# A recurrence whose first step loads into memory of its own, with late loads moved to another queue

## The chip, the core and the metric

The kernel runs on one core of one Trainium2 chip. The metric is the device time of one execution in microseconds (us); less is better. Before the change the median of 3 runs is 937.24 us (936.47 to 937.66).

Engines are named as in the profile: PE (TensorE), PEld (its weight load), DVE (VectorE), ACT (ScalarE), POOL (GpSimd), SP (SyncE). SP and POOL each issue transfers in the order in which their own instructions stand; an instruction that waits holds up all that stand behind it on its engine.

## What is computed

One layer of an encoder trunk over 512 tokens of width 1024, in float32. The pieces that matter here are the two branches and how they merge:

```python
h = rmsnorm(x); u = h @ w_in          # columns: RWKV-7 | differential attention | two gates
# branch A: one delta-rule scan per direction, 8 heads of 64
def step(state, inp):
    r_t, w_t, k_t, v_t, kk_t, a_t = inp
    sa = einsum('bhij,bhj->bhi', state, -kk_t)
    state = state * w_t + sa[..., None] * (kk_t * a_t) + v_t[..., None] * k_t
    return state, einsum('bhij,bhj->bhi', state, r_t)
y = scan(forward) + scan(reverse)     # then group norm, bonus, gate, projection -> A
# branch B: (softmax(Q1 K1) - lam * softmax(Q2 K2)) V, per-head norm, projection -> B
x = x + (sigmoid(gate_a) * A + sigmoid(gate_b) * B) @ w_out
x = x + relu(rmsnorm(x) @ w_ff1)**2 @ w_ff2
x = x + sigmoid(rmsnorm(x) @ w_pg) * (p @ w_pp)
out = rmsnorm(x)
```

## The kernel before

Every dense product is made in three passes of split operands (high times high, low times high, high times low), so a weight block of 512 KB is loaded (`raw`, line 127), split by ACT into `whi` (L131) and by DVE into `wlo` (L135), and used by 24 matmuls of 128x512 (L245 to L247, or L655 where PE's order is chained by hand). The blocks stream through three `raw` buffers on SP's queue in the order of a list.

The stages follow each other: projections and the preparation of the scans; differential attention; the scans, which the code calls the sequence; the merge (`ya`, then `wout`); the two feed-forward products; the last gate and norm. Stages that leave PE waiting are filled with dense matmuls of gates: `gA` in the attention, `gB` in the sequence.

The scan is done in chunks of 64 tokens, 8 per direction, so the sequence has 8 steps `i`, each with the two directions `d` side by side; direction 1 walks the chunks backwards. A step needs three loads from DRAM, all on POOL's queue: `sga` (1 MB, made by `chunk`, L916 to L921), `stt` (the 64x64 inverses of 8 heads, 128 KB, L1032) and `srv` (the values, in partitions 64 to 127 of a tile whose lower half the step fills in later, L1034). The inverses are completed late: `corner_blocks` (L872 to L912) makes their corner blocks on PE in the last part of the attention and writes them to DRAM (`td<-z`, L912), four small writes for each direction.

Within a step (`step`, L1045 to L1098) PE forms `al` from `sga` and the values (and, from the second step on, the state `S`); ACT and DVE copy it to `B` (L1059, L1060); PE multiplies by the inverses into `ss` (L1066); ACT and DVE copy that into the lower half of `srv` (L1067, L1068); PE makes the update of the state (`ss<-srv,sga`) and the output (`yy`), which DVE and ACT carry into `S` and `ya`. After the first stage of each step one half of a `gB` block (12 matmuls) is put in between, and in the first step one half more behind `B`.

Memory decides when a load may start. Pools are stacked on two sides. The tiles of the attention lie in the pool `at`, which is given up when the attention's last product, the projection `yb` of its output (high part `oTh`, low part `oTl`), has read them; `yp` and `seq` (`sq_` in the code) are opened after `at` is closed, on the same side and so in its memory. Each direction has a `tt` and an `rv` tile of its own in `sq_`, two deep, allocated by `slot` (L1025). `kq` and `kq2` lie on the other side: `kq` holds `kT` and later the `k` tile of the chunks, `kq2` (opened at tile `t == 10` of the attention's loop) one chunk buffer.

Loads of three other things wait for their turn on SP's queue between the weight blocks: `bvt` (1 MB, L1138), `g2` (256 KB, L1159) and eight `gA` gates (256 KB each, L1203), which the merge needs; the `gA` tile has three buffers, so the fourth load waits for the first tile's last reader.

Of the kernel before, what the change touches and what calls it, by code (L numbers as in the profile page):

```python
# [10 lines left out]
F32 = mybir.dt.float32  # L11
F32R = mybir.dt.float32r
# [4 lines left out]
P = 128  # L17
# [61 lines left out]
def moved(a):  # L79

    return a.rearrange("p (h t) -> p t h", h=2)
# [28 lines left out]
class Weights:  # L110
# [34 lines left out]
    def next(self, *key):  # L145
        assert UNITS[self.cur] == key, (UNITS[self.cur], key)
        self.prefetch(1 + self.AHEAD)
        w = self.ready[self.cur]
        self.ready[self.cur] = None
        self.cur += 1  # L150
        return w
# [3 lines left out]
def tile_hybrid_encoder(ctx, tc, xT, wts, par, cst_a, cst_p, lor, lqk, nfin, out, dbg=None):  # L155
# [492 lines left out]
    def chained(f, *args, **kw):  # L648

        nonlocal last_pe  # L650
        if last_pe is None:
            last_pe = f(*args, **kw)
        else:
            with tc.issue_after(last_pe.ins):
                last_pe = f(*args, **kw)  # L655
# [81 lines left out]
    def gates():  # L737
        for f in range(GE, GA0):
            yield from gate(f, at, range(8))

        for f2 in range(4):
            wh, wl = W.next("dao", f2)
            for i in range(2):
                ps = psd.tile([P, T], F32, tag="d", name=f"yb{f2}{i}")
                for k in range(4):
                    wk = slice(k * 256 + i * P, k * 256 + i * P + P)
                    for j, (a, b) in enumerate(((wh, oTh), (wh, oTl), (wl, oTh))):
                        chained(nc.tensor.matmul, ps, a[:, wk], moved(b[:, k, :]), start=(k == 0 and j == 0), stop=(k == 3 and j == 2))
                    if k == 3:
                        if not mB:  # L750
                            mB.extend(gp.tile([P, 4, T], F32, tag=f"m{j}", name=f"mB{j}", bufs=1) for j in range(2))
                        nc.scalar.activation(mB[f2 // 2][:, 2 * (f2 % 2) + i, :], ps, AF.Copy)
                    yield
# [3 lines left out]
    def fillk(n, wait=False):  # L757
        nonlocal done
        for _ in range(n):
            if done >= 8 * (GA0 - GE) + 32:  # L760
                return
            next(early_gates)
            done += 1
            if not wait:
                gated()
# [146 lines left out]
                nc.gpsimd.dma_start(tdb[g, 0:H, vs, H:C], x_[rows[g]])  # L912

    early = {}

    def chunk(i, d):  # L916

        own, tag = (kq, "hl"[d] + str(i % 3)) if i % 3 < 2 else ((kq2, "h2"), (kq, "k"))[d]
        ga = own.tile([P, 4, 512], F32, tag=tag, name=f"sga{i}{d}", bufs=1)
        nc.gpsimd.dma_start(ga, gad[d * NCH + (i if d == 0 else NCH - 1 - i)])  # L920
        return ga  # L921

    corners = corner_blocks()
    o_ = at.tile([P, 4, T], F32, tag="qk", name="o_", bufs=1)
# [4 lines left out]
    for t in range(NT + 1):  # L929
        if t > 2:  # L930
            values((t - 3) // 2, (0, 1) if t % 2 == 1 else (2, 3))
        if t + 3 < NT:
            scores(t + 3)
        fillk(AFS[t] if done < AFT else 0, True)
        if t > 0:
            turned(t - 1)
        if t + 2 < NT:
            exps(t + 2)
        if t + 1 < NT:
            weigh(t + 1)  # L940
        if t < NT:
            turn(t)
        gated()
        if t in EC:
            if t == EC[-1]:
                kq2 = pool("kq2")
            for d in range(1 if t == EC[-1] else 2):
                early[EC.index(t), d] = chunk(EC.index(t), d)
        next(diag, None)
        if t == CT:  # L950
            next(corners)
    W.AHEAD = AH2
    fillk(AF2)
    values(NT // 2 - 1, range(4))
    fillk(AF3)
# [23 lines left out]
    selb = at.tile([4, 4, P], F32R, tag="e1", name="selb", bufs=3)  # L979
    nc.scalar.activation(selb, ident[0:4, 0:4, None].broadcast_to([4, 4, P]), AF.Copy)  # L980
    oTh = at.tile([P, 4, T], F32R, tag="q", name="oTh", bufs=1)
    oTl = kq.tile([P, 4, T], F32R, tag="k", name="oTl", bufs=1)
    for hd in range(4):
        ps = psm.tile([P, T], F32, tag="sc", name=f"rb{hd}", bufs=4)
        for i, t_ in enumerate((roh, rol)):
            chained(nc.tensor.matmul, ps, selb[:, hd, :], t_, start=(i == 0), stop=(i == 1))
        on = at.tile([P, T], F32, tag="e0", name=f"on{hd}", bufs=3)
        nc.vector.scalar_tensor_tensor(on, o_[:, hd, :], sub8, ps, ALU.mult, ALU.mult)
        nc.scalar.activation(oTh[:, hd, :], on, AF.Copy)
        nc.vector.tensor_tensor(oTl[:, hd, :], on, oTh[:, hd, :].bitcast(F32), ALU.subtract)  # L990

# [28 lines left out]
            with tc.issue_after(seq_last.ins):  # L1022
                seq_last = nc.tensor.matmul(*args, **kw)  # L1023

    def slot(kind, shape, i, d, n):  # L1025
        return sq_.tile(shape, F32, tag=f"{kind}{d}{i % n}", name=f"s{kind}{i}{d}", bufs=1)

    def load(i, d):
        c = i if d == 0 else NCH - 1 - i
        ga = early.pop((i, d), None) or chunk(i, d)  # L1030
        tt_ = slot("tt", [C, 8, C], i, d, 2)
        nc.gpsimd.dma_start(tt_, tdv[d * NCH + c])  # L1032
        rv = slot("rv", [P, 8, C], i, d, 2)
        nc.gpsimd.dma_start(rv[C:P].rearrange("p u e -> p (u e)"), vd[c * C:(c + 1) * C])  # L1034
        return ga, tt_, rv


# [2 lines left out]
    S = [sq_.tile([P, 4, 2, C], F32, name=f"S{d}") for d in range(2)]  # L1040
    for d in range(2):
        nc.gpsimd.memset(S[d], 0.0)
    early[2, 1] = chunk(2, 1)

    def step(i, d):  # L1045

# [8 lines left out]
            for p, hh in units:  # L1055
                seq_mm(al[half(hh), p, :], ga[:, p, 384:448], S[d][:, p, hh, :], start=False, stop=(p == 3))
        yield
        B = sq_.tile([C, 4, 2, C], F32, tag=f"B{d}", name=f"B{i}{d}", bufs=1)
        nc.scalar.activation(B[:, :, 0, :], al[half(0)], AF.Copy)  # L1059
        nc.vector.tensor_copy(B[:, :, 1, :], al[half(1)])  # L1060
        yield
# [71 lines left out]
    dense = dense_work()  # L1133
    for i in range(NCH):
        steps = [step(i, d) for d in range(2)]
        if i == NCH // 2:
            with tc.issue_after(W.sent.ins):
                nc.sync.dma_start(bvt, bvd.rearrange("a q t -> q a t"))  # L1138
        for st_ in range(6):
            for g in steps:  # L1140
                next(g)
            if st_ == 0 or (i, st_) == (0, 2):
                fill(1)
    pss.close_()
    sq_.close_()
    kq2.close_()
# [7 lines left out]
    mean = sq_.tile([P, 4, 8], F32, name="mean")  # L1154
    var = sq_.tile([P, 4, 8], F32, name="var")
    g2 = sq_.tile([P, 512], F32, name="g2")
    sent = W.sent.ins
    with tc.issue_after(sent):
        nc.sync.dma_start(g2, lor[:, 2, :])  # L1159
    gps = []  # L1160
    yps = [psm.tile([P, T], F32, tag="m", name=f"yps{p}") for p in range(4)]
    for tt in range(4):
# [32 lines left out]
    for f2 in range(4):  # L1195
        w = W.next("wo", f2)
        for i in range(2):
            f = 2 * f2 + i
            ps = psd.tile([P, T], F32, tag="d", name=f"ya{f}")
            dense_fm(w, ps, 4, ygh, ygl, f0=i * P, fw=256)  # L1200
            gA = yp.tile([P, T], F32, tag="gA", name=f"gAt{f}", bufs=3)
            with tc.issue_after(sent):
                nc.sync.dma_start(gA, gad_[f])  # L1203
            nc.vector.scalar_tensor_tensor(gA, gA, 1.0, ps, ALU.add, ALU.mult)
            nc.vector.tensor_tensor(gA, gA, mB[f // 4][:, f % 4, :], ALU.add)
            dump("mg", gA, f)
            nc.scalar.activation(halves(mh[:, f, :]), turns(gA), AF.Copy)
            nc.vector.tensor_tensor(halves(ml[:, f, :]), turns(gA), halves(mh[:, f, :].bitcast(F32)), ALU.subtract)
# [276 lines left out]
```

## Time and profile before

| | before |
|---|---|
| median of 3 runs | 937.24 us (936.47 to 937.66) |
| the profiled execution: its own time / its span | 939.69 us / 937.9 us |
| PE busy, PEld busy | 884.5 us (94%), 741.7 us (79%) |
| DVE, ACT, POOL busy | 570.4 us (61%), 431.0 us (46%), 51.7 us (6%) |
| mean granted clock of PE | 0.976 of full speed |
| chain that ended last: PE, DVE, ACT, issue, DMA | 65%, 15%, 8%, 5%, 5% |
| moved by SP's queue, by POOL's queue | 114.09 MB, 23.60 MB |

The span is what the profiler saw between the first and the last instruction. An execution's own time is 1.8 us longer here, and the profiled execution is 2.45 us above the median of the runs. Busy time says which engine has work; the chain that ended last says what the end waited for, step by step.

### The profile page before, as it was taken

The page shows a single profiled execution, that of the slowest core. Times are in us where ns is not written, and L with a number is a line of the kernel's source. Part 1 is how long each engine was busy: PE and PEld are TensorE (multiplying, and loading weights), DVE is VectorE, ACT ScalarE, POOL GpSimd, SP SyncE. Part 2 cuts the span into 40 slices and gives each one's busy share as a digit, 9 for nine tenths or more (in the row PEclk, how much of TensorE's full clock was granted, in tenths as well). Part 3 has the DMA queues.
Part 4 walks back from the last instruction along what each step waited for, and adds up shares of the span by engine and source line. Part 5 has one row for each costly group of instructions (what it writes and reads, how often), then busy time and mean ns, then how long its engine had stood idle before and what let it go on. Part 6 is the DMA issues. An engine that isn't in the chain of part 4 may idle for free.

```text
span 937.9 us, 14083 instructions
## 1 busy us (share of the span) xinstructions
PE 884.5 (94%) x5640; PEld 741.7 (79%) x5640; DVE 570.4 (61%) x873; ACT 431.0 (46%) x677; POOL 51.7 (6%) x74
## 2 busy tenths in 40 slices
PE   5899898999999996899999999999999999999995
PEld 3788777788567785788877888888888888888884
DVE  7756999769985521467897665554354445334453
ACT  6665555453577531332464544542153235213555
POOL 5000000010000012322000000000000000000000
PEclk9989999999899997899999999999999999999998
DMA  5534788795245258586125423232323232323502
GB/s 214 186 113 146 255 262 265 246 372 164 90 151 123 81 145 244 169 292 209 33 80 192 143 90 104 99 109 94 110 93 113 90 113 90 113 91 111 201 25 90
DMA packets 65553, 138.58 MB, mean 148 GB/s; under 512 B 25808, under 2 KB 28112, under 8 KB 63184
## 3 DMA queue, kind: packets, MB, share of 16 engines
q1 hardware_dynamic: 61248, 114.09, 37.3%
q0 software_dynamic: 4240, 23.60, 7.5%
q8 instruction: 44, 0.72, 0.3%
q14 instruction: 21, 0.17, 0.1%
HBM read 106.73 MB, written 30.93 MB: 147 GB/s over the span
## 4 chain that ended last, share of the span: by engine, by line
PE 65%; DVE 15%; ACT 8%; issue 5%; DMA 5%; SPq 1%; POOL 0%; POOLq 0%; DVEq 0%; ACTq 0%
PE f L246 12%; PE f L247 12%; PE f L245 12%; PE gA L655 4%; DVE wlo L135 2%; PE ss L1023 2%; PE yy L1023 2%; PE sc L655 2%; PE ov L655 1%; DMA md<-ga 1%; ACT whi L131 1%; DMA mi<-md 1%; PE wout L246 1%; DVE mi L580 1%; PE wout L247 1%
## 5 line engine op out<-in xcount | busy, mean ns | idle before, releaser
L131 ACT ACTIVATE whi<-raw 128x1024 fp32r<-128x1024 f32 x134 | 141.4, 1057 | 288.9 <-PE f L246 182.8
L135 DVE TENSOR_TENSOR wlo<-raw,whi 128x1024 fp32r<-128x1024 f32 x134 | 166.8, 1247 | 51.9 <-ACT whi L131 51.0
L247 PE MATMUL f<-fh,wlo 128*128 128x512 f32 x256 | 97.2, 380 | 0.0
L246 PE MATMUL f<-fl,whi 128*128 128x512 f32 x256 | 97.1, 379 | 0.0
L245 PE MATMUL f<-fh,whi 128*128 128x512 f32 x256 | 97.1, 379 | 0.0
L245 PE MATMUL f<-h1h,whi 128*128 128x512 f32 x256 | 97.0, 379 | 0.0
L246 PE MATMUL f<-h1l,whi 128*128 128x512 f32 x256 | 97.0, 379 | 0.0
L247 PE MATMUL f<-h1h,wlo 128*128 128x512 f32 x256 | 97.0, 379 | 0.0
L1262 DVE TENSOR_TENSOR x<-x,f 128x512 f32<-128x512 f32 x32 | 22.0, 687 | 89.5 <-PE f L247 89.5
L1251 DVE SCALAR_TENSOR_TENSOR ft<-f,rf 128x512 f32<-128x512 f32 x32 | 22.1, 691 | 63.5 <-PE f L247 63.4
L245 PE MATMUL in<-hhi,whi 128*128 128x512 f32 x128 | 51.0, 399 | 7.5 <-ACT whi L131 7.5
L246 PEld LDWEIGHTS f<-h1l,whi 128*128 128x128 f32 x256 | 48.4, 189 | 6.9
L245 PEld LDWEIGHTS f<-h1h,whi 128*128 128x128 f32 x256 | 48.4, 189 | 6.9
L247 PEld LDWEIGHTS f<-h1h,wlo 128*128 128x128 f32 x256 | 48.4, 189 | 6.9
L245 PEld LDWEIGHTS f<-fh,whi 128*128 128x128 f32 x256 | 48.4, 189 | 6.8
L247 PEld LDWEIGHTS f<-fh,wlo 128*128 128x128 f32 x256 | 48.4, 189 | 6.8
L246 PEld LDWEIGHTS f<-fl,whi 128*128 128x128 f32 x256 | 48.4, 189 | 6.8
L246 PE MATMUL in<-hlo,whi 128*128 128x512 f32 x128 | 50.9, 397 | 2.1 <-DVE hlo L301 2.1
L247 PE MATMUL in<-hhi,wlo 128*128 128x512 f32 x128 | 50.3, 393 | 1.1 <-DVE wlo L135 1.1
L245 PEld LDWEIGHTS in<-hhi,whi 128*128 128x128 f32 x128 | 25.3, 198 | 11.1 <-ACT whi L131 7.5
L246 PEld LDWEIGHTS in<-hlo,whi 128*128 128x128 f32 x128 | 25.3, 197 | 7.6 <-DVE hlo L301 4.3
L1254 DVE TENSOR_TENSOR h1l<-ft,h1h 128x512 fp32r<-128x512 f32 x32 | 25.7, 804 | 8.7 <-ACT h1h L1253 8.7
(362 smaller groups left out, 1840.0 us busy)
## 6 DMA issues: line engine op xcount, KB each, us to landing
raw<-in_wts_dram SPq DMA_DIRECT2D x134, 512.0 KB, 3.5
gad<-ga SPq DMA_DIRECT2D x16, 1024.0 KB, 5.6
sga<-gad POOLq DMA_DIRECT2D x16, 1024.0 KB, 7.7
xs<-in_xT_dram SPq DMA_DIRECT2D x8, 256.0 KB, 5.5
ppd<-pps SPq DMA_DIRECT2D x2, 1024.0 KB, 5.7
md<-ga SPq DMA_DIRECT2D x32, 64.0 KB, 4.9
gates<-go SPq DMA_DIRECT2D x8, 256.0 KB, 2.1
mi<-md POOLq DMA_DIRECT2D x1, 2048.0 KB, 12.7
```

What stands on the lines that cost most here:

```text
L131: a = nc.scalar.activation(hi, raw, AF.Copy)
L135: b = nc.vector.tensor_tensor(lo, raw, hi.bitcast(F32), ALU.subtract)
L245: nc.tensor.matmul(ps, lh, moved(rh), start=first, stop=False)
L246: nc.tensor.matmul(ps, lh, moved(rl), start=False, stop=False)
L247: return nc.tensor.matmul(ps, ll, moved(rh), start=False, stop=last)
L580: behind[e] = f(*args, **kw)
L655: last_pe = f(*args, **kw)
L1023: seq_last = nc.tensor.matmul(*args, **kw)
L1251: nc.vector.scalar_tensor_tensor(t_, ps, 0.0, rf, ALU.max, ALU.mult)
L1254: nc.vector.tensor_tensor(halves(hl_[:, f, :]), turns(t_), halves(hh_[:, f, :].bitcast(F32)), ALU.subtract)
L1262: nc.vector.tensor_tensor(x[:, f, :], x[:, f, :], ps, ALU.add)
```

## The change

Five things are done:

- `rv` of even steps moves from `sq_` into `kq2`, and the loads of step 0 (both directions) are issued in the attention's loop at `t == 10`, by a new helper `values_in`.
- `tt` moves from `sq_` into `kq2`; the two directions of a step share one tile, direction 0 in partitions 0 to 63 and direction 1 in 64 to 127. `B` lies in the same partitions as the inverses that it is multiplied with.
- `oTl`, the low part of the attention's output, moves out of `kq`'s tile `k` into two tiles of `at`. The tile `k` is then free when `kT` was last read, and the chunk of step 2, direction 1, is issued behind the attention's loop instead of behind the clearing of `S`.
- `bvt`, `g2` and the eight `gA` loads move from SP's queue to POOL's, behind the last chunk.
- The code that allocated `tt` and `rv` per direction (`slot`) is gone.

```diff
-                    for j, (a, b) in enumerate(((wh, oTh), (wh, oTl), (wl, oTh))):
-                        chained(nc.tensor.matmul, ps, a[:, wk], moved(b[:, k, :]), ...)
+                    for j, (a, b) in enumerate(((wh, oTh[:, k]), (wh, oTl[k // 2][:, k % 2]), (wl, oTh[:, k]))):
+                        chained(nc.tensor.matmul, ps, a[:, wk], moved(b), ...)
...
+    last_chunk = None
     def chunk(i, d):
...
-        nc.gpsimd.dma_start(ga, gad[d * NCH + (i if d == 0 else NCH - 1 - i)])
+        nonlocal last_chunk
+        last_chunk = nc.gpsimd.dma_start(ga, gad[d * NCH + (i if d == 0 else NCH - 1 - i)])
         return ga
+
+    rvs = {}
+
+    def values_in(i, d):
+        c = i if d == 0 else NCH - 1 - i
+        rv = (sq_ if i % 2 else kq2).tile([P, 8, C], F32, tag=f"rv{d}{i % 2}", name=f"srv{i}{d}", bufs=1)
+        nc.gpsimd.dma_start(rv[C:P].rearrange("p u e -> p (u e)"), vd[c * C:(c + 1) * C])
+        return rv
...
             for d in range(1 if t == EC[-1] else 2):
                 early[EC.index(t), d] = chunk(EC.index(t), d)
+            if t == EC[-1]:
+                rvs.update({(0, d): values_in(0, d) for d in range(2)})
...
     W.AHEAD = AH2
+    early[2, 1] = chunk(2, 1)
     fillk(AF2)
...
-    oTl = kq.tile([P, 4, T], F32R, tag="k", name="oTl", bufs=1)
+    oTl = [at.tile([P, 2, T], F32R, tag="pdT", name=f"oTl{i}", bufs=2) for i in range(2)]
...
-    def slot(kind, shape, i, d, n):
-        return sq_.tile(shape, F32, tag=f"{kind}{d}{i % n}", name=f"s{kind}{i}{d}", bufs=1)
+    tts = {}
     def load(i, d):
         c = i if d == 0 else NCH - 1 - i
         ga = early.pop((i, d), None) or chunk(i, d)
-        tt_ = slot("tt", [C, 8, C], i, d, 2)
+        rv = rvs.pop((i, d), None) or values_in(i, d)
+        if d == 0:
+            tts[i] = kq2.tile([P, 8, C], F32, tag=f"tt{i % 2}", name=f"stt{i}", bufs=1)
+        tt_ = tts[i][half(d)]
         nc.gpsimd.dma_start(tt_, tdv[d * NCH + c])
-        rv = slot("rv", [P, 8, C], i, d, 2)
-        nc.gpsimd.dma_start(rv[C:P].rearrange("p u e -> p (u e)"), vd[c * C:(c + 1) * C])
         return ga, tt_, rv
...
-    early[2, 1] = chunk(2, 1)
...
-        B = sq_.tile([C, 4, 2, C], F32, tag=f"B{d}", name=f"B{i}{d}", bufs=1)
+        B = sq_.tile([P, 4, 2, C], F32, tag=f"B{d}", name=f"B{i}{d}", bufs=1)[half(d)]
...
-        if i == NCH // 2:
-            with tc.issue_after(W.sent.ins):
-                nc.sync.dma_start(bvt, bvd.rearrange("a q t -> q a t"))
...
+    with tc.issue_after(last_chunk.ins):
+        nc.gpsimd.dma_start(bvt, bvd.rearrange("a q t -> q a t"))
...
-    sent = W.sent.ins
-    with tc.issue_after(sent):
-        nc.sync.dma_start(g2, lor[:, 2, :])
+    with tc.issue_after(last_chunk.ins):
+        nc.gpsimd.dma_start(g2, lor[:, 2, :])
...
-            with tc.issue_after(sent):
-                nc.sync.dma_start(gA, gad_[f])
+            with tc.issue_after(last_chunk.ins):
+                nc.gpsimd.dma_start(gA, gad_[f])
```

The order of PE's, DVE's and ACT's instructions is the same in both kernels; what moves stands on POOL and SP, at two places.

The first place is POOL's queue at the passage from the attention to the sequence. A name ends in the step and the direction (`srv01` is step 0, direction 1; `stt0` serves both directions of step 0); `z01` and `z11` are the corner blocks of direction 0 and of direction 1. Before:

```order
L920 DMA sga20_2568<-gad_119 128x2048
L912 DMA td_121<-z01_2982 32x16x32 x4
L912 DMA td_121<-z11_3089 32x16x32 x4
L920 DMA sga21_3279<-gad_119 128x2048
L1032 DMA stt00_3259<-td_121 64x8x64
L1034 DMA srv00_3261<-vd_124 64x512
L1032 DMA stt01_3263<-td_121 64x8x64
L1034 DMA srv01_3265<-vd_124 64x512
L1032 DMA stt10_3267<-td_121 64x8x64
L1034 DMA srv10_3269<-vd_124 64x512
L1032 DMA stt11_3271<-td_121 64x8x64
L1034 DMA srv11_3273<-vd_124 64x512
```

And in the changed kernel:

```order
L922 DMA sga20_2568<-gad_119 128x2048
L931 DMA srv00_2570<-vd_124 64x512
L931 DMA srv01_2572<-vd_124 64x512
L922 DMA sga21_2727<-gad_119 128x2048
L912 DMA td_121<-z01_2989 32x16x32 x4
L1048 DMA stt0_3266<-td_121 64x8x64
L1048 DMA stt1_3271<-td_121 64x8x64
L912 DMA td_121<-z11_3096 32x16x32 x4
L1048 DMA stt0_3266<-td_121 64x8x64
L1048 DMA stt1_3271<-td_121 64x8x64
L931 DMA srv10_3269<-vd_124 64x512
L931 DMA srv11_3273<-vd_124 64x512
```

The values of step 0 and the chunk `sga21` stand ahead of the corner blocks' writes now, the inverses of direction 0 between the writes of the two directions, and only the values of step 1 at the end.

The second place is the passage from the sequence to the merge. Before, the three kinds of late loads stand on SP among the weight blocks:

```order
L127 DMA raw47_4015<-in_wts_dram 128x1024
L1138 DMA bvt_3252<-bvd_125 128x4x512
L127 DMA raw48_4322<-in_wts_dram 128x1024
L1159 DMA g2_4450<-in_lor_dram 128x512
L1203 DMA gAt0_4687<-gates_123 128x512
L1203 DMA gAt1_4706<-gates_123 128x512
L1203 DMA gAt2_4731<-gates_123 128x512
L127 DMA raw49_4561<-in_wts_dram 128x1024
```

In the changed kernel they stand on POOL, behind the loads of the last step:

```order
L922 DMA sga71_4309<-gad_119 128x2048
L931 DMA srv71_4311<-vd_124 64x512
L1048 DMA stt7_4307<-td_121 64x8x64
L1155 DMA bvt_3259<-bvd_125 128x4x512
L1170 DMA g2_4443<-in_lor_dram 128x512
L1214 DMA gAt0_4680<-gates_123 128x512
L1214 DMA gAt1_4699<-gates_123 128x512
L1214 DMA gAt2_4724<-gates_123 128x512
L1214 DMA gAt3_4743<-gates_123 128x512
```

SP issues weight blocks alone in that part of the program now; the remaining `gA` loads follow on POOL.

## Rows read from the trace of the kernel before

**Rows 1.** The page's 40 equal slices: busy tenths of PE, its granted clock.

```profile
PE   5899898999999996899999999999999999999995
...
PEclk9989999999899997899999999999999999999998
```

**Rows 2.** Stretches: length, busy us (count) by engine, clock, DMA share, GB/s.

```profile
360.00:380.00 20.00, 9.66 (x81) 7.30 (x79) 4.18 (x7) 2.86 (x6) 6.32 (x11) 0.66 0.79 224
...
400.00:420.00 20.00, 19.46 (x408) 17.17 (x408) 12.43 (x28) 7.49 (x19) 6.60 (x11) 1.00 0.83 275
...
380.00:384.00 4.00, 3.68 (x65) 3.64 (x66) 2.21 (x6) 0.79 (x3) 0.31 (x1) 0.57 0.60 165
...
442.00:449.00 7.00, 7.00 (x127) 6.58 (x123) 4.72 (x11) 0.76 (x2) 0.00 (x0) 0.53 0.24 78
```

**Rows 3.** The chain that ended last at 361 us: start, us, what.

```profile
360.98 9.63 DMA srv<-vd
```

**Rows 4.** PE in order of time, step 0: start, us, instruction, idle before it.

```profile
358.27 0.38 PE L245 MATMUL gB<-hhi,whi 128*128 128x512 f32 x1
...
369.03 1.12 PE L1023 MATMUL al<-srv,sga 64*64 64x64 f32 x16 [8.01 <-DMA srv<-vd]
...
377.02 1.15 PE L1023 MATMUL ss<-B,stt 64*64 64x64 f32 x32
380.32 1.98 PE L1023 MATMUL ss<-srv,sga 128*64 128x64 f32 x32 [2.15 <-DVE srv L1068]
...
383.84 0.48 PE L245 MATMUL gB<-hhi,whi 128*128 128x512 f32 x1
```

**Rows 5.** DVE in order of time: the copies that step 0 waits for.

```profile
379.75 0.77 DVE L1068 COPY srv<-ss 64x256 f32<-64x256 f32 x2
```

**Rows 6.** PE in order of time, step 2 and the start of step 3.

```profile
400.54 0.67 PE L1023 MATMUL ss<-B,stt 64*64 64x64 f32 x14 [0.54 <-DVE B L1060]
...
402.88 1.18 PE L1023 MATMUL ss<-srv,sga 128*64 128x64 f32 x32
...
404.93 0.48 PE L245 MATMUL gB<-hhi,whi 128*128 128x512 f32 x1
...
407.71 0.68 PE L1023 MATMUL al<-srv,sga 64*64 64x64 f32 x16
408.32 0.39 PE L1023 MATMUL al<-S,sga 128*64 128x64 f32 x6
```

**Rows 7.** PE in order of time, step 6: a stand, and the next gate block.

```profile
441.69 1.11 PE L1023 MATMUL ss<-B,stt 64*64 64x64 f32 x14 [0.99 <-DVE B L1060]
...
448.97 0.48 PE L245 MATMUL gB<-hhi,whi 128*128 128x512 f32 x1
```

**Rows 8.** POOL in order of time: corner writes, first loads, last load of the sequence.

```profile
335.21 2.57 POOL L912 DMA_DIRECT2D td<-z  x4 [5.54 <-ACT z L906]
358.51 0.57 POOL L920 DMA_DIRECT2D sga<-gad  x1 [20.73 <-PE yb L655]
...
437.22 0.54 POOL L1034 DMA_DIRECT2D srv<-vd  x1 [0.82 <-issue]
```

**Rows 9.** All transfers by line: queue, count, KB each, median us to landing.

```profile
stt<-td POOLq DMA_DIRECT2D x16, 128.0 KB, 5.7
...
td<-z POOLq DMA_DIRECT2D x8, 64.0 KB, 2.6
```

**Rows 10.** The last gA loads: SP's issue, DVE's use, landing between 488 and 510.

```profile
499.86 2.69 SPq L1203 DMA_DIRECT2D gAt<-gates  x2
...
505.86 0.68 DVE L1204 SCALAR_TENSOR_TENSOR gAt<-gAt,ya 128x512 f32<-128x512 f32 x1
...
gAt<-gates SPq DMA_DIRECT2D x5, 256.0 KB, 2.6
```

**Rows 11.** POOL's issue of the value loads: shortest, median, longest ns.

```profile
L1034 POOL DMA_DIRECT2D srv<-vd x16: 522/531/540, 359.8 to 437.2; - x16
```

**Rows 12.** PE in order of time: the last readers of `kT`.

```profile
287.88 1.13 PE L655 MATMUL sc<-kT,qT 64*128 64x512 f32 x4
```

More of the change, by code (lines that the diff above doesn't have):

```diff
@@ L746, in gates @@
                     wk = slice(k * 256 + i * P, k * 256 + i * P + P)
-                    for j, (a, b) in enumerate(((wh, oTh), (wh, oTl), (wl, oTh))):
-                        chained(nc.tensor.matmul, ps, a[:, wk], moved(b[:, k, :]), start=(k == 0 and j == 0), stop=(k == 3 and j == 2))
+                    for j, (a, b) in enumerate(((wh, oTh[:, k]), (wh, oTl[k // 2][:, k % 2]), (wl, oTh[:, k]))):
+                        chained(nc.tensor.matmul, ps, a[:, wk], moved(b), start=(k == 0 and j == 0), stop=(k == 3 and j == 2))
                     if k == 3:
@@ L989, in tile_hybrid_encoder @@
         nc.scalar.activation(oTh[:, hd, :], on, AF.Copy)
-        nc.vector.tensor_tensor(oTl[:, hd, :], on, oTh[:, hd, :].bitcast(F32), ALU.subtract)
+        nc.vector.tensor_tensor(oTl[hd // 2][:, hd % 2, :], on, oTh[:, hd, :].bitcast(F32), ALU.subtract)
     fillk(C0)
```

## The prediction

> **What bounds the kernel now.** I read the slices of the page first, then stretches, then the chain, then the engines one by one in the place that the chain names. The slices [rows 1] show PE at 9 tenths nearly everywhere: time is won only where PE stands or runs at the lower of its two clock levels (1.2 instead of 2.4 GHz). The deepest dip, in PE and in its clock, is slice 16, which lies between 352 and 375 us. The stretch 360 to 380 [rows 2] says it in numbers: PE is busy 9.66 of 20 us, at a granted clock of 0.66, while DMA is busy 0.79 of the time; 400 to 420, the same kind of work two steps later, has 19.46 us at 1.00. The chain of waits [rows 3] names what ends last there: a value load `srv`, 9.63 us from its issue to its use. PE in order of time [rows 4] shows the stand: the gate block that fills the passage begins at 358.27, and the first `al` starts at 369.03 after 8.01 us of waiting for `srv<-vd`. POOL's order [rows 8] says why the load was late: it stood for 20.73 us until the attention's last product (`yb`) gave its memory free at 358.51, and then chunk, inverses and values went out together.
>
> Step 0 has a second loss. The product `ss<-srv,sga` starts at 380.32 after a stand of 2.15 us [rows 4], because DVE copies what it needs only at 379.75 [rows 5], behind work on a gate. In 380 to 384 the clock is at 0.57 again [rows 2], so `ss` and `yy` take 383.84 - 380.32 = 3.52 us [rows 4]; in step 2, at the full clock, the same two take 404.93 - 402.88 = 2.05 us [rows 6].
>
> **The change, part by part.** *Values, inverses and chunk of the first step.* I lay step 0 out anew from 358.27, with durations at the full clock, since PE no longer stands before it. A gate half lasts 407.71 - 404.93 = 2.78 us up to the next group's start [rows 6]: the first `al` starts at 361.05. Sixteen `al` take 408.32 - 407.71 = 0.61 us [rows 6], both directions 1.22: 362.27. The second gate half: 365.05, where the product with the inverses starts. From its start to that of `ss<-srv,sga` it was 380.32 - 377.02 = 3.30 us [rows 4]; that is DVE's and ACT's time, and their order has not moved: 368.35. Then `ss` and `yy`: 2.05 us at the full clock, or 3.52 if it falls in the stand. The next gate half starts at 370.40 or 371.87, instead of 383.84 [rows 4].
>
> *Which of the two.* The clock fell in both places near here where PE stood in the midst of small products: in the stand before 380.32, and in step 6, where after a stand of 0.99 us [rows 7] it is 0.53 for the next seven us [rows 2]. In the changed kernel the stand of step 0 is as long and lies between the same products. I take the fall: 371.87, a saving of 383.84 - 371.87 = **11.97 us**. The Trainium skill (TensorE: Matmul & The Clock Gate, section "Why this matters for your kernels") warns only of longer stands than this one; by it the clock would stay at 2.4 GHz and the saving be 13.44 us. The row speaks against the page, so that is a rival below.
>
> *Are the data there?* Values of step 0 and `sga21` stand on POOL where it was idle. The inverses of direction 1 are the last: corner writes issued at 335.21 for 2.57 us [rows 8], landed 2.6 us later, two issues of some 0.6 each like their neighbours [rows 8], landing 5.7 [rows 9]: 347.3, with 17.8 us to spare before 365.05. The values of step 1 still wait for the attention's memory: 358.51, two issues, and 5.7 as for a load of the same size [rows 9] make 365.3, while step 1 needs them at 371.87 + 2.78 = 374.65. Steps 1 to 7 stay as they are: each load there is issued behind the same readers as before, and those come 12 us sooner together.
>
> *Shared tile, `B` in its partitions.* The products are as many and as large; `al` reads the upper partitions already at the same rate. Nothing. A buffer is free only when both directions have read it, 0.6 us later for direction 0, and its reload has a step's time. Nothing.
>
> *`oTl` in `at`.* DVE's first write to the second tile waits for the last of the small `rb` matmuls instead of the last but one pair; its reader comes far behind. Nothing, and if that cover were gone, the 0.2 us of one matmul.
>
> *Late loads on POOL.* Ten more issues on POOL, ten fewer on SP, about 0.54 us each [rows 11], some 5.4 us on an engine that is busy 6% of the span, behind its last load of the sequence at 437.22 [rows 8], now about 425. `bvt`, `g2` and three `gA` find their memory free; step 7's gate alone began 448.97 - 437.22 = 11.75 us behind that point [rows 7, 8], more than the longest landing on the chain, 9.63 [rows 3], and the merge comes later still. The last five `gA` wait for a buffer. The tightest is the last: SP issued it at about 502.2 (the end of its row less one issue), it took 2.6 us, so 504.8, and DVE used it at 505.86 [rows 10]: 1.0 us to spare. On POOL it may take between the 2.6 us of `td<-z` and the 5.7 of `stt` [rows 9]. I take the lower, since POOL's queue is empty by then while `stt` ran among chunks: cost nothing; the upper makes it 2.1 us late, and the same again for the load that uses its buffer before it, 4.2 us together.
>
> A page speaks against this part. The Trainium skill (SBUF — State Buffer, section "SBUF: two separate sides") says that loads issued by GpSimd are held up while VectorE runs in a mode that locks the port they share, and advises the other queues. Here 16 loads took 522 to 540 ns to issue [rows 11] beside a DVE that was busy 12.43 of 20 us [rows 2], so the rows show no such hold; by the page the gA would be late, as in the second rival.
>
> The sum is made against the profiled execution, whose span is 937.9 us and whose own time, 939.69, lies 2.45 above the median. Taken from the median: 937.24 - 11.97 = **925.3 us**.
>
> **The rivals.** *The clock does better.* If it holds in step 0, the saving is 13.44: 923.8. If the clock's fall also fails to come in step 6, there are 448.97 - 441.69 = 7.28 us [rows 7] against 404.93 - 400.54 = 4.39 for the same products [rows 6], 2.89 more: 920.9. For it: everything ahead is at another time, and a stand of 0.54 us at 400.54 [rows 6] cost no clock. Against: both stands keep their causes. Chance 0.25.
>
> *The last `gA` come late on POOL.* By the bound above up to 4.2 us, 925.3 to 929.5. Chance 0.06.
>
> *The clock stays low for longer in step 0*, as in step 6 (2.89 us instead of 3.52 - 2.05 = 1.47): 926.7. Chance 0.08.
>
> *The change does not do all it says:* the first `al` waits, through the shared tile or the pool it lies in, for loads that still go out at 358.51. They land at 365.3 instead of 361.05, 4.2 us lost: 929.5. Against it stands the order, in which the first step's loads come ahead. Chance 0.05.
>
> *The chunk holds up the corners: slower.* `sga21` now stands on POOL ahead of `td<-z`. It waits for the last readers of `kT`. Those are the scores that end at 287.88 + 1.13 = 289.0 [rows 12], long before the corner blocks. If its memory came free only with `yb` at 358.51, as now, then the issue (0.57), both sets of writes (2 x 2.57), their landings (2 x 2.6), four issues of 0.6 and a landing of 5.7 [rows 8, 9] would follow, 19.0 us: the inverses at 377.5, step 0 over at 377.5 + 3.30 + 3.52 = 384.3 instead of 383.84, and 9.63 [rows 3] instead of 5.7 for the landing adds 3.9: 937.7 to 941.6. It costs time as soon as the chunk is released after 365.05 - 19.0 = 346, and makes the kernel slower from about 358 on. Chance 0.04.
>
> **How the numbers follow.** The forecast has 0.52, the rivals 0.25, 0.06, 0.08, 0.05 and 0.04. The range 921.5 to 928.5 takes in the forecast, the clock that holds in step 0, the longer fall and half of the late `gA`; outside are the clock that holds in both places (some 0.06), the rest of the late loads, the first step that waits and the held corners, 0.18 in all. A measurement of this kernel can tell about 0.2%, 1.9 us, from no change. All cases but the last are faster by far more: faster 0.95, same 0.01, slower 0.04.
>
> **What would show it.** PE in order of time should go from the gate half to `al` with no stand near 361, and the granted clock be 1.00 until `ss<-srv,sga`; then a stand of about 2 us for DVE's copies, and a stretch of low clock. The next gate half should begin near 372. POOL should write the corners by 338 as before, with inverses between the two sets, and issue the values of step 1 at 358.5. From step 1 on each step should be as long as before, step 6's stand and low clock included, and the merge about 12 us earlier, with no new wait of DVE for `gA`. The prediction is wrong if `al` still waits for a load, if POOL stands at `sga21` beyond 346, or if the merge is stretched by more than 2 us.

## The result, and the profile after

| | before | after |
|---|---|---|
| median of the comparison | 937.45 us (4 runs, 936.47 to 939.11) | 924.34 us (4 runs, 923.27 to 927.08) |
| ratio, 95% interval | | 0.9859 [0.9832, 0.9887] |
| profiled execution: own time / span | 939.69 / 937.9 us | 924.65 / 922.5 us |
| PE, DVE, POOL busy | 884.5, 570.4, 51.7 us | 879.3, 572.0, 57.2 us |
| mean granted clock of PE | 0.976 | 0.985 |
| moved by SP's queue, by POOL's | 114.09, 23.60 MB | 110.68, 27.01 MB |

The kernel is faster by 13.1 us; the forecast was 925.3 us. The page's slices of the changed kernel, busy tenths of PE and its granted clock:

```profile
PE   5999898899999998999999999999999999999995
...
PEclk9999999999999999998999999999999999999998
```

The dip of slice 16 [rows 1] is gone. But for the last slice, which had it before too, one dip of the clock is left, in slice 19 (415 to 438 us), and that is step 6. PE in order of time from the end of the attention (start, us, instruction, idle before it), the rows that answer to [rows 4] and [rows 7]:

```profile
356.06 0.38 PE L655 MATMUL yb<-oTh,wlo 128*128 128x512 f32 x1
356.28 0.38 PE L245 MATMUL gB<-hhi,whi 128*128 128x512 f32 x1
...
358.96 1.15 PE L1037 MATMUL al<-srv,sga 64*64 64x64 f32 x32
...
362.83 0.98 PE L1037 MATMUL ss<-B,stt 64*64 64x64 f32 x32
366.24 1.15 PE L1037 MATMUL ss<-srv,sga 128*64 128x64 f32 x32 [2.44 <-DVE srv L1081]
367.19 1.13 PE L1037 MATMUL yy<-srv,sga 128*64 128x64 f32 x32
368.25 0.48 PE L245 MATMUL gB<-hhi,whi 128*128 128x512 f32 x1
...
426.54 1.10 PE L1037 MATMUL ss<-B,stt 64*64 64x64 f32 x14 [0.99 <-DVE B L1073]
...
433.83 0.48 PE L245 MATMUL gB<-hhi,whi 128*128 128x512 f32 x1
```

`al` follows its gate half without a wait. The stand for DVE's copies is there, 2.44 us instead of 2.15, but `ss` and `yy` behind it now take 368.25 - 366.24 = 2.01 us, not 3.52. From the first gate half to the third it is 368.25 - 356.28 = 11.97 us, where it was 383.84 - 358.27 = 25.57 [rows 4]: 13.60 us saved in this one place. Two more rows of the kernel before belong beside [rows 4], its last `yb` and its second gate half:

```profile
358.05 0.38 PE L655 MATMUL yb<-oTh,wlo 128*128 128x512 f32 x1
...
371.71 0.79 PE L245 MATMUL gB<-hhi,whi 128*128 128x512 f32 x1
```

They show that the wait cost more than its own length. Before, the clock was at 0.50 from 364 to 376 us, and the gate half behind `al` took 377.02 - 371.71 = 5.31 us, where it now takes 362.83 - 360.04 = 2.79. Of the 13.60 us saved, 8.08 lie ahead of the start of `al`, 1.60 from there to this gate half, 2.52 in it and 1.51 in `ss` and `yy`; the stretch between `ss<-B,stt` and `ss<-srv,sga` grew by 0.11. Stretches of the changed kernel (length, busy us and count by engine PE, PEld, DVE, ACT, POOL, then clock, DMA share, GB/s), beside [rows 2]:

```profile
360.00:380.00 20.00, 16.74 (x321) 14.55 (x318) 10.79 (x23) 6.96 (x18) 5.44 (x10) 1.00 0.54 190
...
364.00:366.00 2.00, 0.00 (x0) 0.00 (x0) 1.97 (x3) 0.83 (x3) 1.38 (x2) 1.00 0.20 61
427.00:433.00 6.00, 6.00 (x106) 5.65 (x104) 3.96 (x9) 0.75 (x2) 0.00 (x0) 0.50 1.03 382
```

PE is idle from 364 to 366 and keeps its full clock; in step 6, behind a stand of 0.99 us, it works for six us at half of it, as before. DVE in order of time shows what the copies stand behind:

```profile
362.93 0.69 DVE L1122 TENSOR_TENSOR gb<-gB,rbs 128x512 f32<-128x512 f32 x1 [1.94 <-PE gB L247]
363.81 1.22 DVE L135 TENSOR_TENSOR wlo<-raw,whi 128x1024 fp32r<-128x1024 f32 x1 [0.18 <-ACT whi L131]
364.95 0.68 DVE L1124 SCALAR_TENSOR_TENSOR mB<-gb,mB 128x512 f32<-128x512 f32 x1
365.66 0.77 DVE L1081 COPY srv<-ss 64x256 f32<-64x256 f32 x2
```

POOL in order of time, beside [rows 8]: values and chunk early, inverses between the corner writes, only step 1's values behind `yb`, the late loads behind the last step's.

```profile
275.82 1.06 POOL L931 DMA_DIRECT2D srv<-vd  x2
285.72 0.57 POOL L922 DMA_DIRECT2D sga<-gad  x1 [8.84 <-PE sc L655]
...
333.22 2.57 POOL L912 DMA_DIRECT2D td<-z  x4 [1.02 <-ACT z L906]
339.06 1.36 POOL L1048 DMA_DIRECT2D stt<-td  x2 [3.27 <-DMA td<-z]
356.74 1.07 POOL L931 DMA_DIRECT2D srv<-vd  x2 [16.32 <-PE yb L655]
...
423.24 0.78 POOL L1155 DMA_DIRECT2D bvt<-bvd  x1
...
487.37 0.54 POOL L1214 DMA_DIRECT2D gAt<-gates  x1 [1.78 <-DVE ml L1219]
```

The rest moved little. From step 1's `al` to step 7's it was 451.76 - 386.63 = 65.13 us and is 436.62 - 371.04 = 65.58; from there to the end 486.14 and 485.88. Ahead of the sequence, where PE's work is the same, the last `yb` starts at 356.06 instead of 358.05. These 2 us are not shown to be the change's: in the fourteen traces of this study that matmul starts anywhere from 354.0 to 365.6 us, and the mean granted clock of the first 350 us is 0.99 in the two earliest and 0.96 in the latest. So beside each median I give the time from the start of the last `yb` to the end of the span: 937.9 - 358.05 = 579.85 us before and 922.5 - 356.06 = 566.44 after, **13.41 us** less.

### The profile page after: what moved, and what is told of

Same layout as the page of the kernel before. It is cut to its first block, busy times and chain, and to the rows that moved or that the text cites. A ratio compares the mean times of both kernels' runs of the same rounds, so it can differ in the third digit from the quotient of the medians.

```text
span 922.5 us, 14089 instructions
## 1 busy us (share of the span) xinstructions
PE 879.3 (95%) x5640; PEld 738.1 (80%) x5640; DVE 572.0 (62%) x873; ACT 430.7 (47%) x677; POOL 57.2 (6%) x84
## 3 DMA queue, kind: packets, MB, share of 16 engines
q1 hardware_dynamic: 59424, 110.68, 36.6%
q0 software_dynamic: 5232, 27.01, 8.8%
## 4 chain that ended last, share of the span: by engine, by line
PE 69%; DVE 16%; ACT 7%; DMA 4%; issue 3%; SPq 1%; POOLq 0%; DVEq 0%; ACTq 0%
PE f L246 12%; PE f L247 12%; PE f L245 12%; PE gA L655 4%; DVE wlo L135 2%; PE yb L655 2%; PE ss L1037 2%; PE yy L1037 2%; PE sc L655 2%; PE ov L655 2%; DMA md<-ga 1%; PE wout L246 1%; DVE mi L580 1%; ACT whi L131 1%; PE wout L245 1%
```

## The experiments

My theory: the first step waited because two things met. Its values had to wait for the attention's memory, and then landed slowly because chunk, inverses and late loads (1, 0.5 and 2 MB) went out in the same microseconds. The rivals: the memory alone, or the queue alone. The first seven runs take parts back, or do one alone. The ratio is to the kernel before as it ran beside the run in question, on the same chip: its median was 935.88 us for the first four rows below "after", 937.87 for the next four and 938.66 for the last four; so the ratios of different rows compare better than the medians. "Passage" is the time from the first gate half of step 0 to the third (to the fourth, where a half was added).

| kernel | median us | ratio to before, 95% | passage | last `yb` to end |
|---|---|---|---|---|
| before | | | 25.57 | 579.85 |
| after | 924.34 | 0.9859 [0.9832, 0.9887] | 11.97 | 566.44 |
| values late | 924.30 | 0.9883 [0.9853, 0.9914] | 12.67 | 566.74 |
| inverses late | 922.67 | 0.9871 [0.9826, 0.9916] | 11.98 | 567.34 |
| before, queue only | 933.04 | 0.9967 [0.9946, 0.9988] | 23.14 | 577.10 |
| late loads on SP | 923.84 | 0.9864 [0.9828, 0.9899] | 11.98 | 566.26 |
| before, values only | 929.74 | 0.9933 [0.9907, 0.9959] | 16.07 | 571.54 |
| values late, late loads on SP | 933.75 | 0.9951 [0.9928, 0.9973] | 20.89 | 575.52 |
| chunk back | 922.35 | 0.9865 [0.9806, 0.9924] | 13.42 | 565.61 |
| copies first, means behind step 7 | 924.72 | 0.9857 [0.9823, 0.9892] | 12.71 | 566.81 |
| after, again | 922.14 | 0.9831 [0.9787, 0.9876] | 11.98 | 566.32 |
| copies first, means behind step 6 | 925.27 | 0.9852 [0.9810, 0.9895] | 11.16 | 562.63 |
| half gate in the stand | 927.21 | 0.9854 [0.9809, 0.9898] | 12.25 | 564.61 |
| both of the last two | 926.00 | 0.9857 [0.9818, 0.9896] | 12.26 | 567.86 |

**Values late.**

```diff
-        rv = (sq_ if i % 2 else kq2).tile([P, 8, C], F32, ...)
+        rv = sq_.tile([P, 8, C], F32, ...)
...
-            if t == EC[-1]:
-                rvs.update({(0, d): values_in(0, d) for d in range(2)})
```

> The changed kernel, with step 0's values taken back into the attention's memory, so that POOL may issue them only behind the last yb (356.3 us in the trace of the change); the inverses, the chunk and the late loads stay as changed. Theory A, the memory alone made the wait: the four loads of values go out between 356.7 and 358.8 and land about 10 us later, as the load of 360.98 did before (9.63); the first al waits until about 366 or 367 instead of 358.96, TensorE's clock falls as before, and most of the gain goes back: 932 to 937 us. Theory B, memory and traffic made it together (before, 3 MB of late loads and chunk and the inverses went out in the same microseconds, which here they do not): the values land in 2.6 to 4 us, as the loads of step 1's values do in the trace of the change (2.6), the first al waits until 359.5 to 361, and the loss is 0.5 to 2.5 us: 925 to 927 us. Theory C, it is the inverses or the queue and not the values: 924 us, no stand.

The stands at `al` are 0.26 and 0.15 us:

```profile
363.59 0.68 PE L1035 MATMUL al<-srv,sga 64*64 64x64 f32 x16 [0.26 <-DMA srv<-vd]
364.42 0.68 PE L1035 MATMUL al<-srv,sga 64*64 64x64 f32 x16 [0.15 <-DMA srv<-vd]
```

Theory A falls; B is right, and its price even smaller than I gave: 0.7 us in the passage, 0.3 behind `yb`.

**Inverses late.**

```diff
-            tts[i] = kq2.tile([P, 8, C], F32, ...)
+            tts[i] = sq_.tile([P, 8, C], F32, ...)
```

> The changed kernel, with the shared tile of the inverses taken back into the attention's memory, so that the two loads of step 0's inverses go out behind the last yb, first in POOL's queue (356.7 and 357.4); the values stay early. They are wanted at 362.83. Theory A (a late load takes about 10 us whatever else moves): they land near 367, ss waits some 4 us and the clock may fall: 928 to 931 us. Theory B (the landing time is the traffic's): such a load landed 2.6 us after its issue when little else moved and 5.7 us at the middle, so 360 to 363, beside 1 us of stand at most: 924 to 925.5 us.

No wait for `stt` in the trace; the four loads landed in 4.3 us at the median, and the passage is as in the changed kernel. B again. The 0.9 us more behind `yb` lie in later steps.

**Before, with the queue alone changed.**

```diff
-        if i == NCH // 2:
-            with tc.issue_after(W.sent.ins):
-                nc.sync.dma_start(bvt, ...)
...
+    with tc.issue_after(last_chunk.ins):
+        nc.gpsimd.dma_start(bvt, ...)
```

(and the same for `g2` and `gA`)

> The kernel before, with nothing changed but the queue of the late loads: the bias table, g2 and the merge's gates go from SP to POOL behind the last chunk. Step 0's chunk, values and inverses are issued at 358.5 to 366.5 as before. Theory A (memory alone): the landing of 9.63 us and the stand of 8.01 us stay: 936 to 938 us. Theory B (memory and traffic): without 2 MB of late loads beside them the values of the second direction, issued at 360.98, land in 4 to 6 us, the first al starts at 364 to 366 instead of 369.03, and the run takes 932 to 935 us. Were the traffic all of it, the landing would be 2.6 us and the run 930 us.

The first `al`, which stood for 8.01 us before [rows 4]:

```profile
364.42 1.12 PE L1025 MATMUL al<-srv,sga 64*64 64x64 f32 x16 [4.85 <-DMA srv<-vd]
```

The stand shrank by 3.2 us, and 2.75 us are gained behind `yb`. That is B, but weaker than I gave it: the values of the second direction took 7.54 us and not 4 to 6, while the chunk and the inverses still go out in the same queue.

**Late loads back on SP.**

```diff
-    with tc.issue_after(last_chunk.ins):
-        nc.gpsimd.dma_start(bvt, ...)
+        if i == NCH // 2:
+            with tc.issue_after(W.sent.ins):
+                nc.sync.dma_start(bvt, ...)
```

> The changed kernel with the late loads back on SP's queue, where they were before. Values and inverses of step 0 are on board long before, so their traffic at 356 to 361 meets only step 1's values, which are wanted at 371.04 and would land by 368 even at the 9.63 us of before. Expected: no stand at the first al, 924 us give or take 1.5; POOL's queue was then worth nothing by itself. The rival, that the new queue is a part of the gain (the crowd delays step 1's or the weights' loads): 926 to 930 us. The other rival, that the queue behind the chunks costs something in the merge: 922 us or less, with a wait for gA gone at the output.

No difference that these runs can tell, 566.26 us: with everything else in place the queue is worth nothing, and on POOL it costs nothing.

**Values late and late loads on SP.** Both edits together.

> The changed kernel with two parts taken back at once, of which each alone cost nothing: step 0's values wait for the attention's memory again, and the late loads are back on SP's queue; chunk and inverses stay early. The values go out just behind the last yb beside 2 MB of late loads and a weight. Theory B (memory and traffic): they land in 5 to 8 us instead of 2.55, the first al waits 2 to 5 us, and from the last yb to the end it takes 568.5 to 572 us instead of 566.44; the run takes 926.5 to 930 us. Theory D (the crowd counts only through POOL's own queue, where the chunk and an inverse stood ahead of the values): no more than the 0.4 us of the run with the values late alone: 924 to 925 us, 566.4 to 567.2 from the last yb.

Each alone cost 0.3 and -0.2 us; together they cost 575.52 - 566.44 = 9.08. That is more than I gave, 568.5 to 572 us behind `yb`, since the stand was followed by a low clock. PE in order of time:

```profile
359.80 0.38 PE L245 MATMUL gB<-hhi,whi 128*128 128x512 f32 x1
...
367.12 1.82 PE L1035 MATMUL al<-srv,sga 64*64 64x64 f32 x32 [4.58 <-DMA srv<-vd]
368.87 0.79 PE L245 MATMUL gB<-hhi,whi 128*128 128x512 f32 x1
```

The gate half behind `al` lasts 5.3 us (its first matmul 0.79) instead of 2.79 (0.48). A load of step 0's values, 128 KB in the same memory and issued behind the same `yb`, can be followed through four traces, as the chain that ended last gives it (issue, us to its use; direction 0 in the third, direction 1 in the others). In the kernel before it took 9.63 us [rows 3]. Before with the queue alone changed, so beside chunk and inverses only:

```profile
359.53 7.54 DMA srv<-vd
```

Values late and late loads on SP, so beside the late loads only:

```profile
360.26 6.73 DMA srv<-vd
```

Values late, beside neither:

```profile
361.56 2.72 DMA srv<-vd
```

That settles it, and theory D falls: late loads on the other queue alone made the load 4 us longer. The memory set when the load could start; the traffic of that moment made 2.7 us into 9.6, and the gate half on PE covers about 2.8.

**Before, with the values alone early.** (`values_in` as in the change.)

```diff
+            if t == EC[-1]:
+                rvs.update({(0, d): values_in(0, d) for d in range(2)})
...
-        rv = slot("rv", [P, 8, C], i, d, 2)
-        nc.gpsimd.dma_start(rv[C:P]...)
+        rv = rvs.pop((i, d), None) or values_in(i, d)
```

> The kernel before, with one part of the change alone: step 0's two loads of values go out early into memory of their own. Chunk, inverses and late loads stay where they were before, in the crowd behind the last yb. Theory A (the values are the change): the first al follows the gate half without a wait and the whole gain is there: 923.5 to 925.5 us. Theory B (memory and traffic; every load in the crowd is late): the values are on board, but the four inverses go out at about 359 to 361 beside 3 MB and land in about 9.9 us, the median of before, near 369 on the trace of before, where ss is laid out for 365; so the wait moves from al to ss, some 4 us long, the clock falls there or not, and a half to two thirds of the gain are left: 928 to 932 us. From the last yb to the end that is 566 us by A and 570 to 574 by B (before 579.85, change 566.44).

B: 8.31 of the 13.41 us are gained, and the wait is at the inverses now, a load of which took 9.51 us (the chain, then PE in order of time):

```profile
357.28 9.51 DMA stt<-td
```

```profile
358.46 1.15 PE L1034 MATMUL al<-srv,sga 64*64 64x64 f32 x32
...
365.23 1.12 PE L1034 MATMUL ss<-B,stt 64*64 64x64 f32 x16 [2.84 <-DMA stt<-td]
...
366.92 1.12 PE L1034 MATMUL ss<-B,stt 64*64 64x64 f32 x16 [0.57 <-DMA stt<-td]
```

**Chunk back.**

```diff
-    oTl = [at.tile([P, 2, T], F32R, tag="pdT", ...) for i in range(2)]
+    oTl = kq.tile([P, 4, T], F32R, tag="k", name="oTl", bufs=1)
...
     W.AHEAD = AH2
-    early[2, 1] = chunk(2, 1)
...
         nc.gpsimd.memset(S[d], 0.0)
+    early[2, 1] = chunk(2, 1)
```

> The changed kernel with the last early chunk taken back: the output's low halves lie in the K tile again, so that the chunk goes out behind the last yb, ahead of step 1's values, with the late loads behind it. Only step 2 wants the chunk, 25 us later, and step 1's values are wanted 14 us later. Expected: no difference, 924 us give or take 1, and 566.4 us give or take 0.5 from the last yb. Rival, that the megabyte holds up step 1's values or the weights: 925.5 us or more, with a wait at step 1.

No wait for chunk or values, 565.61 us and a median of 922.35, both a little below what I gave: this part is worth nothing while the others stand. Its trace shows something else. Behind the same stand of 2.44 us the clock fell:

```profile
375.77 1.98 PE L1036 MATMUL ss<-srv,sga 128*64 128x64 f32 x32 [2.44 <-DVE srv L1081]
377.50 1.80 PE L1036 MATMUL yy<-srv,sga 128*64 128x64 f32 x32
379.23 0.48 PE L245 MATMUL gB<-hhi,whi 128*128 128x512 f32 x1
```

`ss` and `yy` took 379.23 - 375.77 = 3.46 us, and the passage 13.42 us instead of 11.97. The time behind `yb` is below that of the changed kernel all the same, since step 6 took 11.68 us here instead of 14.28.

**Copies first.** The last five runs ask what the two stands that are left are worth, and what the clock does there. `tails` collects each gate's last step; `copied` is the step's last copy of `srv`.

```diff
-        gb = yp.tile([P, T], F32, tag="gb", ...)
-        nc.vector.tensor_tensor(gb, ps, rbs, ALU.mult)
...
+        tails.append((f, ps))
...
+            with tc.issue_after(copied.ins):
+                nc.vector.tensor_tensor(gb, ps, rbs, ALU.mult)
...
+            if st_ == 3:
+                finish_gates()
...
+        with tc.issue_after(copied.ins):
+            nc.vector.tensor_reduce(mean[:, tt, :], yt, AX.X, ALU.add)
```

> The changed kernel with DVE's copies of the chain put first: the multiply and the add of each gate of direction B (with its tanh) stand behind the step's last copy of srv, and the merge's means behind the last copies of step 7, so that no B or srv copy waits behind them. Theory: the stand of step 0 shrinks from 2.44 us to 1 to 1.5, those of steps 2 and 4 (0.5 us) go, and in step 6 the stands of 0.37 and 0.99 us go and with them the fall of the clock, so that it takes 9.6 to 10 us instead of 14.28. From the last yb to the end 560 to 562.5 us instead of 566.44; the run 917.5 to 920.5 us. Rival 1: the clock falls all the same, in step 6 or later: 921.5 to 923. Rival 2: the gate's bank comes free later and the merge's means start 2 to 5 us later, and TensorE waits for one of them behind step 7: 924 us or more.

The first half came out, the sum did not. The stand of step 0 shrank to 1.62 us, step 2 took 9.77 us instead of 10.50 and step 6 10.66 instead of 14.28. But in step 0 the clock fell behind the shorter stand:

```profile
366.66 1.98 PE L1037 MATMUL ss<-srv,sga 128*64 128x64 f32 x32 [1.62 <-DVE srv L1084]
```

Step 4 had a gap of 1.57 us that the profile puts down to nothing, and from step 7's `al` to the end it took 489.06 us instead of 485.88: rival 2, in the main. PE and DVE in one stretch behind step 7:

```profile
445.04:455.04 10.00, 8.65 (x41) 6.46 (x40) 9.86 (x20) 8.73 (x13) 0.00 (x0) 1.00 0.18 54
```

DVE is busy 9.86 of 10 us there, and 9.41 in the like stretch of the changed kernel (446.6 to 456.6 us). PE's stand of 1.35 us for a `gb` in it is not the loss, since the changed kernel stands 1.24 us for one a little later. The largest part of the loss is found where the projection `ya` waits for DVE's work on `gAt`. Waits in the 90 us from step 7 on (us in total, times, longest), in the changed kernel and here:

```profile
PE ya L245 <- DVE gAt L1215: 0.3, 1, 0.3
```

```profile
PE ya L245 <- DVE gAt L1229: 2.8, 3, 1.8
```

**After, again; means behind step 6; a half gate in the stand; both.**

> The changed kernel once more, beside the three that follow. Its execution shows again whether TensorE's clock holds in step 0 behind the stand of 2.44 us. Theory A (the stand's length decides): it holds, step 0 takes 12.08 us as in the trace of the change, and 566.4 us pass from the last yb to the end. Theory B (something else decides, as the runs with the chunk taken back and with the copies first let suppose, where it fell behind 2.44 and 1.62 us): either is possible, 12.1 or 13.5 us. In both cases the run takes 922 to 926 us.

```diff
+                if i == 6:
+                    copied6 = copied
...
-        with tc.issue_after(copied.ins):
+        with tc.issue_after(copied6.ins):
             nc.vector.tensor_reduce(mean[:, tt, :], yt, AX.X, ALU.add)
```

> As the run with the copies first, but the merge's means of the two middle blocks stand behind step 6's last copy, not behind step 7's. There step 6 took 10.66 us instead of 14.28 and step 2 9.77 instead of 10.50, and the merge gave 3.2 us back, since VectorE started its means 15 us later and was busy 9.9 us of 10 behind step 7. Theory: with the means some 4 us earlier than there, 1 to 3 of the 3.2 us come back, step 7 loses up to 0.7: 562 to 565.5 us from the last yb, 919.5 to 923 us. Rival: VectorE's work behind step 7 is too much wherever the means stand, and the merge waits as long as before: 566 to 567 us, 924 us.

```diff
-            if st_ == 0 or (i, st_) == (0, 2):
+            if st_ == 0 or (i, st_) in ((0, 2), (0, 3)):
                 fill(1)
```

> The changed kernel with one half of a gate more ahead of step 0's ss on srv, taken from those that run beside the merge; nothing else is changed. Theory: the half (2.78 us at full clock) covers the stand of 2.44 us, the clock holds in step 0 whatever else is so, step 0 up to step 1's al is 12.08 + 0.3 to 0.5 us long with the half in it, and the merge has 2.7 us less of gates to do: 563.7 to 565 us from the last yb, 921 to 923 us. Rival: the half is wanted beside the merge, where TensorE stands for the means and the last projection already, and the time comes back there: 566.4 us, 924 us.

> Both of the last two together: the half in step 0's stand, and DVE's copies first with the means behind step 6's copies. Theory: the gains add, less what both take of the same stand: 560 to 563.5 us from the last yb, 917 to 921 us. Rival: both draw on the same slack beside the merge, where VectorE and TensorE then wait for each other: 564 us or more.

The changed kernel held its clock in step 0 again. So did the run with the means behind step 6, behind a stand of 1.62 us:

```profile
365.83 1.15 PE L1037 MATMUL ss<-srv,sga 128*64 128x64 f32 x32 [1.62 <-DVE srv L1084]
```

In that run the time behind `yb` is 562.63 us, 3.8 less than after, as expected: the passage and steps 2 and 6 are shorter (11.16, 9.77, 10.40 us) and the end is only 0.7 longer. The half gate covers the stand (no wait before `ss`, clock at full) and 564.61 us are left. Both together lose: 567.86, with a gap of 2.34 us in step 4 that no row explains and 489.37 us from step 7 to the end: the rival. None of this shows in the medians, and all three lie above what I gave. In this comparison the changed kernel ran at 922.14 us (919.87 to 929.92), the three others at 925.27 (920.82 to 930.06), 927.21 (918.60 to 929.93) and 926.00 (922.65 to 929.64), and the intervals overlap. What two traces gain behind `yb` is smaller than what executions differ by ahead of it, so no version is shown to beat the changed kernel, and whether the 3.8 us are real in the mean stays open.

## Why the prediction was right

- **What bounded the kernel** was read rightly: the stand for a load in slice 16. The saving is in that passage, and nowhere else of size.
- **The layout of step 0.** Gate half, `al`, second half: forecast 1.22 us for `al` and 2.78 for a half; measured 360.04 - 358.96 = 1.08 and 2.79. From `ss` to `ss<-srv,sga` forecast 3.30 us, measured 366.24 - 362.83 = 3.41. The third half was laid out 12.13 us behind the first with the clock at full and 13.60 with the fall; measured 11.97. (That 11.97 and 13.60 also stand for the saving, forecast and measured, is chance.)
- **The step that failed** is "I take the fall". The clock held at 1.00 through a stand of 2.44 us, so the saving in this passage is 13.60 us, not 11.97: the term of the sum was 1.6 us too small, most of it the clock's 1.47. The first rival, 923.8 us, was the right one for step 0 and is nearer to the measured 924.34 than my 925.3. The range took in both, so the number being right does not speak for the fall. The Trainium skill (TensorE: Matmul & The Clock Gate, section "Why this matters for your kernels") would have let the clock stand there, and the trace of the change agrees with it. But the runs do not make that a rule: with the same stand of 2.44 us it held in five traces, both of the changed kernel itself among them, and fell in one, which took 13.42 us, close to my 13.60; with 1.62 us it held in one and fell in one. What I passed over is that the fall I took my case from came some 11 us after a stand of 8.01 us. In all four traces where PE stood 2.8 us or more for a load in step 0 (before, queue only, values only, values late with late loads on SP), `ss` and `yy` ran at a low clock and took 3.2 to 3.5 us; of the eight without that stand, but with the one for the copies, six held. Whether the earlier stand is the reason is not shown.
- **Step 6** was forecast as before, stand and low clock, and in this trace it was: 14.28 us in both. In the later runs the same two stands (0.37 and 0.99 us) went with 11.4 to 14.3 us, in the repeat of the changed kernel with 12.81; that this step came out as forecast was partly luck.
- **Data in time.** The last inverses went out at 339.06 for 1.36 us, and the four loads of that time took 5.1 us at the median, so they had about 18 us to spare; step 1's values went out at 356.74 as soon as `yb` let them, and nothing waited. "Nothing" for the shared tile, for `B` and for `oTl` held: `yb` and the steps are as long as before, within 0.4 us.
- **Late loads on POOL** cost nothing, but narrowly. Transfers of the last part of the merge (queue, count, KB each, median us to landing) and DVE's use of the last, beside [rows 10]:

```profile
gAt<-gates POOLq DMA_DIRECT2D x5, 256.0 KB, 2.9
...
490.75 0.68 DVE L1215 SCALAR_TENSOR_TENSOR gAt<-gAt,ya 128x512 f32<-128x512 f32 x1
```

  The last was issued at 487.37, landed about 490.3 by this median, and DVE used it at 490.75 without a wait. The issue took 0.54 us beside a busy DVE, as [rows 11] had it. The Trainium skill (SBUF — State Buffer, section "SBUF: two separate sides") has such loads held only while VectorE runs in a mode that locks the port they share; the trace shows no hold, but no run shows which mode VectorE was in, so "by the page the gA would be late" in the prediction says more than the page does. Putting the loads back on SP changed the time behind `yb` by 0.2 us.
- **What I did not see.** The prediction costed every part by itself and gave the queue nothing, which is right only beside the others. In the kernel before, the queue alone gave 2.75 us and the values alone 8.31; in the changed kernel, either could be taken back for nothing, and both together cost 9.08.

## What to carry to other kernels

A load that is late has two causes, when it may start and what else is moving then; follow the one load through versions before pricing a part, because two parts that hide the same wait can each be taken back for nothing (0.3 and -0.2 us here) while both together are worth 9.08. Where executions differ by more than an edit is worth, measure from a landmark just ahead of the edit to the end, and still let the medians decide. Putting a VectorE copy that TensorE waits for ahead of other work shortened the stand for it, but what is put behind the copy must still fit where it lands: of the two versions one gained 3.8 us behind `yb` and one nothing, and no median shows a gain.

## What was not expected of the hardware

- Whether PE's clock falls in a given stand is not set by the stand's length: 1.62 us with a fall and 2.44 us without, between the same products. What else decides is open.
- The low clock also wanders ahead of the sequence. In the repeat of the changed kernel the only low stretch between 20 and 350 us, in steps of 10 us, is at 40 to 60 (0.77 and 0.89); in the run with the chunk back there are more, down to 0.66 at 250 to 260 and 0.55 at 320 to 330, and the last `yb` starts at 365.59 instead of 354.48, for the same products.
- PE had gaps inside steps 1 to 6 that are put down to no other engine and no load ("issue"): one of 0.74 us in the trace of before and one of 0.82 in that of after, but up to three, of up to 2.34 us, in most later traces. Their cause is open.
